# Moving the transposed activations to a pool behind the hidden tiles, at the weights' place modulo 4096 bytes

## The chip, the cores and the metric

The kernel runs on one core of one Trainium2 chip. The metric is the time of one execution on the device in microseconds. Three executions of the kernel before took 2161.57, 2165.28 and 2165.72 us; the median is 2165.28 us.

## The reference

Two layers of a hybrid block work on 256 tokens of width 2048, all in float32. Each layer does the following:

```python
h = rmsnorm(x, g_mix[l])
proj = h @ w_in[l]                       # 2048 -> 3904, split into seven parts
out_a = rglru_group(...)                 # gated linear recurrence, width 768
out_b = diff_attention_group(...)        # 4 heads, two softmaxes, width 512
out_c = mla_group(...)                   # 6 heads over a low-rank query and key/value, width 768
x = x + concatenate([out_a, out_b, out_c]) @ w_out[l]
h = rmsnorm(x, g_ffn[l])
x = x + (silu(h @ w_gate[l]) * (h @ w_up[l])) @ w_down[l]    # 2048 -> 5632 -> 2048
```

A last rmsnorm follows. Nearly all of the arithmetic is in the products with w_in, w_out, w_gate, w_up and w_down.

## The kernel before

**The split matmul.** Every float32 operand of a large product is held as two parts in the matmul format float32r: a high part, which is the rounded value, and a low part, which is the rest. A product is then three matmuls into one accumulator (`mm3`, lines 209 to 211): high by high, high by low, low by high. The first argument of `nc.tensor.matmul` after the accumulator is the stationary operand, loaded into the array, and the second one is the moving operand, which streams through it.

**The weights.** `load_split` (from line 187) brings a tile of up to 1024 columns of float32 per partition from HBM into one of three buffers of the pool wraw, on SyncE's queue. ScalarE rounds it into `whi` (line 203) and VectorE subtracts to get `wlo` (line 204); both are tiles of the pool whl, with three buffers each. A buffer is loaded again when both have read it.

**The activations.** `build_xT` transposes x on TensorE (line 283) in blocks of 128 by 128, scales it by the norm's gain and splits it into `xTh` and `xTl`, two tiles of 128 partitions by 16 k-slices by 256 tokens that live as long as the kernel. They lie in the pool `const`, between the small tile `half` and `junk`. The hidden activations, the mixed outputs and the normed low-rank inputs are split in the same way into `hTh` and `hTl`, tiles of 4 k-slices by 256 tokens (4096 bytes of a partition each), in the pool `ht` with six buffers of each.

**The order of the pools.** const comes first, then wraw, whl, ht and sm. Each pool follows the one before it in the partition's bytes. const holds ident, x, pv, half, xTh, xTl, junk, warm, pos_i, cst, rsb, the arena (17060 words) and some small tables.

**The products.** `gemm` uses the activations as the stationary side and streams the weights: for each weight tile, each half of 128 tokens, each segment of columns and each k-slice in the tile it issues `mm3`. Gate and up (`k2`) have two k-slices of 512 columns in a tile; w_out and w_down have one k-slice of 1024 columns as two segments of 512; the gemm at C_QA has one k-slice of 832 columns as 512 and 320; the one of w_q_b's rope columns has two k-slices of 384. Each of them gives twelve matmuls for a tile. `gemm_T` does the reverse: the weights are stationary in blocks of 128 columns, and the activations stream, 256 columns at a time. Its right side is xTh and xTl for the LRU's two inputs (768 columns each) and hTh and hTl for the attention's.

TensorE's program order is written out by hand: the generators in `side` and `lazy` (attention heads, transposes, recurrence) are given a turn after each weight tile by `tick`. The other engines' order comes from the scheduler, in which the weight casts and the evacuations have a high priority.

The products on xTh and xTl as the stationary side are the gemm at C_QA, the three at C_DQ, C_DQ + 512 and C_DV, and the eleven blocks of gate and up, in both layers. Those on hTh and hTl are w_out, w_down, the rope columns of w_q_b and the value columns of w_kv_b.

Of the kernel before, what the change touches and what calls it, by code (L numbers as in the profile page):

```python
# [11 lines left out]
F32 = mybir.dt.float32  # L12
F32R = mybir.dt.float32r
# [8 lines left out]
P = 128  # L22
D = 2048
T = 256
NT = 2
DEPTH = 2
KD = D // P
# [27 lines left out]
def body(ctx: ExitStack, tc: tile.TileContext, x_in, pos_in, pvec_in, lamv_in, cst_in, w_in, w_r, w_i, w_q_b,  # L55
         w_kv_b, w_out, w_gate, w_up, w_down, g_final, out):
    nc = tc.nc
    pool = lambda name, bufs=1, **k: ctx.enter_context(tc.tile_pool(name=name, bufs=bufs, **k))
    const = pool("const")
    wraw_p = pool("wraw", 3)  # L60
    whl_p = pool("whl", 3)
    ht_p = pool("ht", 6)
    sm_p = pool("sm", 4)
    acc_p = pool("acc", 5, space=PSUM)
    aux_p = pool("aux", 3, space=PSUM)
# [11 lines left out]
    load_x(0, 256)  # L77
    nc.sync.dma_start(pv, pvec_in)

    half = const.tile([P, 8], F32, name="half")  # L80
    xTh = const.tile([P, KD, T], F32R, name="xTh")
    xTl = const.tile([P, KD, T], F32R, name="xTl")
    junk = const.tile([P, 512], BF16, name="junk")
    warm = const.tile([P, 512], BF16, name="warm")
    nc.vector.memset(warm, 0.0)
    nc.gpsimd.memset(half, -0.5)
    nc.scalar.activation(junk[:, 0:8], half, AF.Exp)
    pos_i = const.tile([P, NT], I32, name="pos_i")
# [835 lines left out]
```

## Time and profile before

| | |
|---|---|
| median of three runs | 2165.28 us (2161.57 to 2165.72) |
| the profiled execution | 2164.01 us |
| its span, first to last instruction | 2162.2 us |
| mean granted TensorE clock | 0.997 of 2.4 GHz |
| TensorE matmul, busy | 2146.5 us (99%), 10302 instructions |
| TensorE weight load, busy | 1783.7 us (82%) |
| VectorE, busy | 1157.1 us (54%) |
| ScalarE, busy | 1003.4 us (46%) |
| moved by DMA | 391 MB, 181 GB/s on average |

The span is counted from the first to the last instruction; the execution's own time is 1.8 us longer. A matmul's duration in the trace runs from its start to the modelled end of its pipeline, so that matmuls overlap; the distance from one start to the next is the pace at which they are worked off. "PEclk" is the share of the full TensorE clock that was granted.

### The profile page before, as it was taken

How to read it: one execution, taken by the hardware profiler on the slowest of the kernel's cores; microseconds unless marked ns; L12 is line 12 of the kernel's file. 1: busy time of each engine (PE TensorE's matmuls, PEld its weight loads, DVE VectorE, ACT ScalarE, POOL GpSimd, SP SyncE). 2: the span in 40 equal slices, each digit the busy share in tenths (PEclk: the TensorE clock that was granted, in tenths of full speed). 3: DMA queues.
4: the chain of work that ended last, by engine and by line, in shares of the span. 5: the costliest groups of instructions: out<-in, count | busy, mean ns of one | idle time of the engine just before them, and what ended most of it. 6: DMA issues, size and time to landing. Idle time of an engine off the chain costs nothing.

```text
span 2162.2 us, 26714 instructions
## 1 busy us (share of the span) xinstructions
PE 2146.5 (99%) x10302; PEld 1783.7 (82%) x10302; DVE 1157.1 (54%) x1497; ACT 1003.4 (46%) x1345; POOL 12.9 (1%) x27
## 2 busy tenths in 40 slices
PE   9999999999999999999999999999999999999998
PEld 8888888888888888888898888888888888888886
DVE  5775755444444444444565757554444444445454
ACT  5764654444443344443447546454444433444443
POOL 0000000000000000000000000000000000000000
PEclk9999999999999999999999999999999999999999
DMA  7564456666665666666565645566666666666655
GB/s 216 172 166 131 151 176 185 185 185 184 185 189 192 193 186 186 185 186 191 181 189 158 180 126 184 178 179 190 182 185 187 191 193 189 186 187 181 189 184 171
DMA packets 183439, 391.14 MB, mean 181 GB/s; under 512 B 19088, under 2 KB 36624, under 8 KB 183184
## 3 DMA queue, kind: packets, MB, share of 16 engines
q1 hardware_dynamic: 183312, 389.45, 60.7%
q8 instruction: 80, 1.31, 0.3%
q14 instruction: 47, 0.39, 0.1%
HBM read 387.30 MB, written 2.10 MB: 180 GB/s over the span
## 4 chain that ended last, share of the span: by engine, by line
PE 98%; DMA 0%; issue 0%; ACT 0%; DVE 0%; SPq 0%; DVEq 0%; POOLq 0%; POOL 0%; ACTq 0%
PE acc L209 31%; PE acc L211 31%; PE acc L210 31%; PE aux L283 2%; PE aux L676 1%; PE aux L675 1%; PE aux L732 1%; DMA wraw<-in_w_in 0%; PE aux L690 0%; PE aux L534 0%; PE aux L533 0%; ACT whi L203 0%; PE aux L691 0%; SPq L75 0%; DVE wlo L204 0%
## 5 line engine op out<-in xcount | busy, mean ns | idle before, releaser
L204 DVE TENSOR_TENSOR wlo<-wraw,whi 128x1024 fp32r<-128x1024 f32 (+2 forms) x756 | 895.4, 1185 | 880.1 <-ACT whi L203 879.0
L203 ACT CAST whi<-wraw 128x1024 fp32r<-128x1024 f32 (+2 forms) x756 | 770.1, 1019 | 1053.4 <-PE acc L211 934.5
L209 PE MATMUL acc<-whi,xTh 128*128 128x512 f32 x1728 | 685.1, 396 | 1.8 <-ACT whi L203 1.0
L210 PE MATMUL acc<-wlo,xTh 128*128 128x512 f32 x1728 | 676.8, 392 | 0.6 <-DVE wlo L204 0.6
L211 PE MATMUL acc<-whi,xTl 128*128 128x512 f32 x1728 | 676.8, 392 | 0.0
L209 PE MATMUL acc<-whi,hTh 128*128 128x512 f32 (+1 forms) x992 | 388.6, 392 | 0.0
L209 PEld LDWEIGHTS acc<-whi,xTh 128*128 128x128 f32 x1728 | 326.1, 189 | 74.8 <-issue 1.3
L211 PEld LDWEIGHTS acc<-whi,xTl 128*128 128x128 f32 x1728 | 325.8, 189 | 73.4
L211 PE MATMUL acc<-whi,hTl 128*128 128x512 f32 (+1 forms) x992 | 385.5, 389 | 0.0
L210 PEld LDWEIGHTS acc<-wlo,xTh 128*128 128x128 f32 x1728 | 326.2, 189 | 71.4 <-DVE wlo L204 0.9
L210 PE MATMUL acc<-wlo,hTh 128*128 128x512 f32 (+1 forms) x992 | 384.8, 388 | 0.0
L209 PEld LDWEIGHTS acc<-whi,hTh 128*128 128x128 f32 x992 | 186.8, 188 | 38.1 <-issue 1.3
L211 PEld LDWEIGHTS acc<-whi,hTl 128*128 128x128 f32 x992 | 186.5, 188 | 38.0
L210 PEld LDWEIGHTS acc<-wlo,hTh 128*128 128x128 f32 x992 | 186.8, 188 | 36.9
L209 PE MATMUL acc<-xTh,whi 128*128 128x256 f32 x384 | 110.6, 288 | 0.2 <-ACT whi L203 0.2
L211 PE MATMUL acc<-xTh,wlo 128*128 128x256 f32 x384 | 108.4, 282 | 0.8 <-DVE wlo L204 0.8
L210 PE MATMUL acc<-xTl,whi 128*128 128x256 f32 x384 | 108.2, 282 | 0.6 <-DVE xTl L293 0.6
L209 PEld LDWEIGHTS acc<-xTh,whi 128*128 128x128 f32 x384 | 72.4, 188 | 2.7 <-issue 1.3
L210 PEld LDWEIGHTS acc<-xTl,whi 128*128 128x128 f32 x384 | 72.4, 189 | 1.1 <-DVE xTl L293 1.0
L211 PEld LDWEIGHTS acc<-xTh,wlo 128*128 128x128 f32 x384 | 72.3, 188 | 1.2 <-DVE wlo L204 1.2
L826 DVE SCALAR_TENSOR_TENSOR arena<-acc,rs,arena 128x512 f32<-128x512 f32 x44 | 32.9, 748 | 42.9 <-PE acc L211 42.9
L283 PE MATMUL aux<-ident,arena 128*128 128x128 f32 x324 | 48.6, 273 | 0.0
(174 smaller groups left out, 868.1 us busy)
## 6 DMA issues: line engine op xcount, KB each, us to landing
wraw<-in_w_gate SPq DMA_DIRECT2D x176, 512.0 KB, 3.7
wraw<-in_w_up SPq DMA_DIRECT2D x176, 512.0 KB, 3.7
wraw<-in_w_down SPq DMA_DIRECT2D x176, 512.0 KB, 4.5
wraw<-in_w_out SPq DMA_DIRECT2D x64, 512.0 KB, 3.8
wraw<-in_w_in SPq DMA_DIRECT2D x64, 384.0 KB, 3.2
wraw<-in_w_in SPq DMA_DIRECT2D x48, 512.0 KB, 3.8
wraw<-in_w_in SPq DMA_DIRECT2D x32, 416.0 KB, 3.4
wraw<-in_w_q_b SPq DMA_DIRECT2D x8, 384.0 KB, 4.0
```

The lines of the kernel that those rows point to most:

```text
L203: nc.scalar.copy(hi[:, :n], raw[:, :n])
L204: nc.vector.tensor_tensor(lo[:, :n], raw[:, :n], hi[:, :n].bitcast(F32), ALU.subtract)
L209: nc.tensor.matmul(ps, a[0], b[0], start=start, stop=False)
L210: nc.tensor.matmul(ps, a[0], b[1], start=False, stop=False)
L211: nc.tensor.matmul(ps, a[1], b[0], start=False, stop=stop)
L283: nc.tensor.transpose(ps[:, d:d + P], s, ident)
L675: nc.tensor.matmul(S[:, c0:c0 + n], qT[:, h, qs], kT[:, h, 0:n], start=True, stop=False)
L676: nc.tensor.matmul(S[:, c0:c0 + n], qrT[b0:b0 + 64, h // 2, qs], krT[b0:b0 + 64, 0:n], start=False, stop=True)
L732: nc.tensor.matmul(S[:, c0:c0 + n], qk[b0:b0 + 64, 0, q * P:(q + 1) * P], qk[b0:b0 + 64, 1, 0:n], start=True, stop=True)
L826: nc.vector.scalar_tensor_tensor(sil[t], ps, rs[0][:, t:t + 1], sil[t], ALU.mult, ALU.mult)
```

## The change

A new pool `xt`, with one buffer, is opened between ht and sm, and xTh and xTl are allocated from it instead of from const. The tile `half` is allocated a few lines later, after `warm`. No instruction is added or removed.

```diff
@@ -60,6 +60,7 @@
     wraw_p = pool("wraw", 3)
     whl_p = pool("whl", 3)
     ht_p = pool("ht", 6)
+    xt_p = pool("xt")
     sm_p = pool("sm", 4)
     acc_p = pool("acc", 5, space=PSUM)
     aux_p = pool("aux", 3, space=PSUM)
@@ -77,12 +78,12 @@
     load_x(0, 256)
     nc.sync.dma_start(pv, pvec_in)
 
-    half = const.tile([P, 8], F32, name="half")
-    xTh = const.tile([P, KD, T], F32R, name="xTh")
-    xTl = const.tile([P, KD, T], F32R, name="xTl")
+    xTh = xt_p.tile([P, KD, T], F32R, name="xTh")
+    xTl = xt_p.tile([P, KD, T], F32R, name="xTl")
     junk = const.tile([P, 512], BF16, name="junk")
     warm = const.tile([P, 512], BF16, name="warm")
     nc.vector.memset(warm, 0.0)
+    half = const.tile([P, 8], F32, name="half")
     nc.gpsimd.memset(half, -0.5)
     nc.scalar.activation(junk[:, 0:8], half, AF.Exp)
     pos_i = const.tile([P, NT], I32, name="pos_i")
```

## Rows read from the trace of the kernel before

**Rows 1.** The page, busy time by engine and the chain's shares by line.
```profile
PE 2146.5 (99%) x10302; PEld 1783.7 (82%) x10302; DVE 1157.1 (54%) x1497; ACT 1003.4 (46%) x1345; POOL 12.9 (1%) x27
...
PE acc L209 31%; PE acc L211 31%; PE acc L210 31%; PE aux L283 2%; PE aux L676 1%; PE aux L675 1%; PE aux L732 1%; DMA wraw<-in_w_in 0%; PE aux L690 0%; PE aux L534 0%; PE aux L533 0%; ACT whi L203 0%; PE aux L691 0%; SPq L75 0%; DVE wlo L204 0%
```
**Rows 2.** Groups by form, TensorE; names are out, moving, stationary; busy us, mean ns.
```profile
L209 PE MATMUL acc<-whi,xTh 128*128 128x512 f32 x1664 | 665.2, 400 | 1.8 <-ACT whi L203 1.0 <-DVE arena L487 0.8
L211 PE MATMUL acc<-whi,xTl 128*128 128x512 f32 x1664 | 657.0, 395 | 0.0
L210 PE MATMUL acc<-wlo,xTh 128*128 128x512 f32 x1664 | 656.8, 395 | 0.6 <-DVE wlo L204 0.6
L209 PE MATMUL acc<-whi,hTh 128*128 128x512 f32 x960 | 377.7, 393 | 0.0
L211 PE MATMUL acc<-whi,hTl 128*128 128x512 f32 x960 | 374.8, 390 | 0.0
L210 PE MATMUL acc<-wlo,hTh 128*128 128x512 f32 x960 | 374.1, 390 | 0.0
L209 PE MATMUL acc<-xTh,whi 128*128 128x256 f32 x384 | 110.6, 288 | 0.2 <-ACT whi L203 0.2
```
**Rows 3.** Timeline of gate and up, start and length in us; 156 matmuls, first and last.
```profile
355.90 0.40 PE L209 MATMUL acc<-whi,xTh 128*128 128x512 f32 x1
...
391.93 0.40 PE L211 MATMUL acc<-whi,xTl 128*128 128x512 f32 x1
```
**Rows 4.** Timeline of a down stretch; 486 matmuls, first and last.
```profile
630.07 0.39 PE L209 MATMUL acc<-whi,hTh 128*128 128x512 f32 x1
...
740.00 0.39 PE L211 MATMUL acc<-whi,hTl 128*128 128x512 f32 x1
```
**Rows 5.** Timeline of the gemm at C_QA; 36 matmuls before the last row.
```profile
55.28 0.39 PE L209 MATMUL acc<-whi,xTh 128*128 128x512 f32 x1
...
55.97 0.31 PE L209 MATMUL acc<-whi,xTh 128*128 128x320 f32 x1
...
56.41 0.39 PE L209 MATMUL acc<-whi,xTh 128*128 128x512 f32 x1
...
62.10 0.39 PE L209 MATMUL acc<-whi,xTh 128*128 128x512 f32 x1
```
**Rows 6.** Timeline of the gemm of w_q_b's rope columns; 24 matmuls, first and last.
```profile
117.32 0.34 PE L209 MATMUL acc<-whi,hTh 128*128 128x384 f32 x1
...
121.32 0.33 PE L211 MATMUL acc<-whi,hTl 128*128 128x384 f32 x1
```
**Rows 7.** Timeline, activations moving: 118 matmuls on xT, then 49 on hT.
```profile
1097.06 0.28 PE L209 MATMUL acc<-xTh,whi 128*128 128x256 f32 x1
...
1110.94 0.28 PE L209 MATMUL acc<-xTh,whi 128*128 128x256 f32 x1
...
1192.17 0.28 PE L210 MATMUL acc<-hTl,whi 128*128 128x256 f32 x1
...
1197.92 0.28 PE L210 MATMUL acc<-hTl,whi 128*128 128x256 f32 x1
```
**Rows 8.** The page's DMA issues: count, KB each, median us to landing.
```profile
wraw<-in_w_gate SPq DMA_DIRECT2D x176, 512.0 KB, 3.7
...
wraw<-in_w_down SPq DMA_DIRECT2D x176, 512.0 KB, 4.5
```
**Rows 9.** Stretches: us, busy of PE, PEld, DVE, ACT, POOL; PEclk, DMA share, GB/s.
```profile
630.00:740.00 110.00, 110.00 (x488) 91.06 (x486) 51.83 (x45) 42.46 (x41) 0.00 (x0) 1.00 0.61 192
445.00:484.00 39.00, 39.00 (x169) 31.61 (x168) 18.49 (x18) 15.96 (x16) 0.00 (x0) 1.00 0.62 180
```
**Rows 10.** Groups in gate and up, 445 to 484 us: the split of the weights.
```profile
L204 DVE TENSOR_TENSOR wlo<-wraw,whi 128x1024 fp32r<-128x1024 f32 x15 | 18.4, 1224 | 20.0 <-ACT whi L203 20.0
L203 ACT CAST whi<-wraw 128x1024 fp32r<-128x1024 f32 x14 | 14.7, 1049 | 22.0 <-PE acc L211 22.0
```
**Rows 11.** A stretch in the attention of the first layer, same columns as rows 9.
```profile
258.00:268.00 10.00, 9.21 (x34) 6.76 (x33) 7.42 (x26) 6.06 (x19) 0.00 (x0) 0.83 0.32 107
```

## The prediction

> **What bounds the kernel now.** I read the page from the top. TensorE is busy for 2146.5 of 2162.2 us, and the chain that ended last is almost only TensorE: three lines, the three products of the split matmul, hold 31% each [rows 1]. No wait stands on that path; the time is the number of matmuls times their pace, plus some 16 us of idle time. So the next view is the one that groups TensorE's work by form, and in it I look for equal shapes with unequal times. There is one pair. The 512-column matmuls whose stationary operand is a slice of xTh or xTl (3 x 1664 = 4992 of them) last 400, 395 and 395 ns; those of the same shape with hTh or hTl (3 x 960) last 393, 390 and 390 [rows 2]. These durations overlap, since matmuls are pipelined, so the pace has to be taken from the timeline, as start to start. In a gate and up stretch with nothing between, the first starts at 355.90 us and the 156th at 391.93: 36.03 us over 155 steps, 232.4 ns each [rows 3]. In a down stretch, 630.07 to 740.00 us are 485 steps: 226.7 ns each [rows 4]. The granted clock is 1.00, the 2.4 GHz level, in stretches of both kinds [rows 9]. So equal work costs 5.7 ns (2.5%) more when xT is the stationary side.
>
> **Is it the stage or the operand?** The two stretches differ in more than the operand: gate and up take two k-blocks of 512 columns per weight tile and give six matmuls in a row to one accumulator, down takes one k-block of 1024 columns and changes the accumulator after three. Two other stages cross this. The first gemm after the LRU input (C_QA, 832 columns as 512 and 320) has down's order with xT: from 55.28 to 62.10 us go six rounds of three 512-column and three 320-column matmuls, 6.82 us or 1.137 us a round. Three of the narrow ones take 56.41 - 55.97 = 0.44 us, which leaves 0.697 us for three wide ones: 232.2 ns each, slow [rows 5]. The gemm of w_q_b has gate's order, two k-blocks a tile, with hT and 384 columns: 4.00 us over 23 steps, 173.9 ns [rows 6]. From 384 to 512 columns at one column per 1/2.4 ns are 53.3 ns more, 227.2 ns: the fast pace. So the order of the stage does not make the pace; the operand goes with it, and what tells xT from hT to TensorE is where it lies.
>
> **Where it lies.** By my count of the allocations (bytes of a partition): ident 512, x 16384, pv 696 and half 32 lie ahead of xTh, so it starts some 1.2 KB past a multiple of 4096. The constants end near 122.7 thousand, some 3.9 KB past one, and there begin wraw (3 x 4096), whl (6 x 4096) and ht (12 x 4096), all whole multiples. So hTh and hTl have the remainder of whi and wlo, and xTh and xTl one about 2.7 KB off. The change takes 32768 bytes, 8 x 4096, out of the constants, so that wraw, whl, ht and the arena keep their remainders, and xT follows ht on the weights' remainder, in bytes (176 to 209 thousand) where hT slots lie now. A slice of 1024 bytes per k, 512 per half of the tokens, gives xT the eight places within 4096 that hT's four k-slices have; the moving sides start at 0 or 2048 in both. Down pairs all eight with both at one pace.
>
> **The sum.**
> - 512-column matmuls on xT: 4992 x (232.4 - 226.7) = 28.5 us less [rows 2 to 4]. The grouped durations give 1664 x (7 + 5 + 5) ns = 28.3 us, a second count from other numbers [rows 2]. Lower end: gate and up alone gain (2 layers x 11 blocks x 16 x 2 x 2 x 3 = 4224), and 5 ns each: 21 us. Upper end: 6.2 ns each, 31 us, half a nanosecond beyond hT's pace; no row shows a lower one.
> - 320 columns, 192 of them: now 146.7 ns [rows 5], and the fast 173.9 ns less 64 columns at 1/2.4 ns is 147.2 [rows 6]. They are on the fast pace already: 0, either end 0.1 us.
> - xT as the moving side, 3 x 384 matmuls of 256 columns [rows 2]: 13.88 us over 117 steps, 118.6 ns, against 119.8 with hT (5.75 us over 48 steps) [rows 7]. Here xT's present place is the better one. If it becomes like hT, 1152 x 1.2 = 1.4 us are lost; the other end is 1.4 us gained, the same difference the other way. I take the loss.
> - The transposes and attention matmuls read x, ident and arena. Their remainders stay (junk and warm alone move by 32 bytes against them), so 0. Were their distance in whole 4096s to count like xT's place, 2.5% of the 2% of the chain in L283 [rows 1] is 1.1 us either way.
> - The builders of xT write the same bytes to another address, and `half` is allocated after warm but filled at the same point: 0, with the first stage's weight wait as cover.
> - What is late next. All of the gain is taken off TensorE, so the weights must come 2.5% faster in gate and up. A 512 KB tile feeds 12 matmuls: 2.79 us now, 2.72 us then. A raw buffer must be filled, cast and subtracted within three tiles, 8.16 us: 3.7 us to landing [rows 8], 1.05 us and 1.22 us [rows 10] leave 2.2 us. The cast's only idle time there, 22.0 us, is ended by TensorE [rows 10], that is, the weights wait for it. Down lives at 2.72 us a tile with 4.5 us to landing [rows 8] and 192 GB/s, where gate and up use 180 [rows 9]. So 0, and what it costs if that fails stands under the rivals. In the attention stages the side work has 0.07 us less per tile; I give it up to 1 us of new idle time, from the 16 us there are.
>
> 28.5 - 1.4 - 0.3 (a part of that last 1 us) = 26.8, say 27 us. The profiled execution took 2164.0 us, 1.8 more than its span; 2164.0 - 27 = 2137 us. It lies 1.3 us under the median of the runs, 2165.28, within their spread of 4 us.
>
> The trace also speaks against a rule here: same shape, same clock, 5.7 ns apart by operand. The Trainium skill, "SBUF — State Buffer", section "SBUF: two separate sides", says of the engines' ports that contention is confined to the pair which VectorE and GpSimd share, and "PE, ACT, and DVE's dedicated pair never wait on anyone." By that rule an address could not cost TensorE anything and the time would stay at 2164; by the rows it does cost.
>
> **The rivals.**
> - *The place does nothing* (2164, chance 0.07). Every slow wide matmul belongs to an xT stage, so something else of those stages could slow the stream: the shorter rows of the weights' transfers, or the activations on ScalarE. For it: no single row shows an address. Against it: the slow pace in the first gemm, which has neither up-projection nor Silu [rows 5]. The port rule of the Trainium skill named above would be this case.
> - *The distance counts too* (2150, chance 0.06). After the move xT lies 13 to 25 times 4096 past the slots of the weights' parts (it lies behind ht's twelve), and hT lay 1 to 17 times past them. If only about half of these distances is fast, half of 28.5 us stays: 2164 - 14 = 2150. Against it: down uses six slots of each part, spread over that whole stretch, at one pace [rows 4].
> - *The weights come late* (slower, 2174, chance 0.04). Place: gate and up, where a row of a transfer is half as long as in down. If a tile's landing takes over 2.2 us longer than now, TensorE idles at the block's start, and an idle stretch can be followed by the 1.2 GHz level: at 258 to 268 us the engine idles for 0.8 us and the granted clock is 0.83 over 10 us [rows 11], 1.7 us lost. One such fall in each of the 22 gate and up blocks costs 37 us: 2164 - 27 + 37 = 2174. It decides against the change from 16 falls on. Against it: the 2.2 us, and a share of the transfer engines of 0.62 here and 0.61 in down [rows 9].
> - *The pool does not land where the words say* (chance 0.03). If a pool started on some other remainder, xT would have a new place with a pace of its own: 2164 if it is as bad as now, more if worse.
>
> **How the numbers follow.** Forecast 0.80; its own range is 2133 to 2141 (31 us less; 22 us less and a clock fall more). The others 0.07, 0.06, 0.04 and 0.03. To leave out no more than 2 in 10 the range goes from 2133 to 2147, which takes in partial gains of 17 us. A measurement here tells about 0.2%, 4.3 us, from no change. Faster: 0.80 + 0.06 = 0.86; within: 0.07 + 0.02 = 0.09; slower: 0.04 + 0.01 = 0.05.
>
> **What would show it.** Right: in the group view, the xT wide matmuls at 393, 390 and 390 ns like hT's; start to start 226.7 ns in gate and up, with no interval of 0.24 us left; the first gemm's round at 1.120 us instead of 1.137; hT stages unchanged; gate and up at some 185 GB/s or more, with the cast still waiting for TensorE. The 256-column stream at 119.8 ns shows the loss of 1.4 us, at 118.6 it did not come. Wrong: the wide xT matmuls still at 232 ns (the place is not the cause), a mixture of both paces by slice (distance), or the casts waiting for DMA and new stretches at the lower clock (late weights).

## The result and the profile after

The changed kernel takes 2139.59 us (median of four runs, 2138.23 to 2141.62) against 2164.28 us before on the same chip. The ratio is 0.989, with a 95% interval of 0.9878 to 0.9903: 24.7 us or 1.1% faster. The forecast was 2137 us, with a range of 2133 to 2147. The profiled execution took 2138.23 us with a span of 2136.4, that is 25.8 us less than 2164.01 and 2162.2 before.

The page after, busy time and the chain by line, to be read against [rows 1]. Lines of the code are one higher than before, so L210 to L212 are the three products of the split matmul.

```profile
PE 2121.6 (99%) x10302; PEld 1780.3 (83%) x10302; DVE 1157.0 (54%) x1497; ACT 1004.1 (47%) x1345; POOL 12.9 (1%) x27
...
PE acc L210 31%; PE acc L212 31%; PE acc L211 31%; PE aux L284 2%; DMA wraw<-in_w_in 1%; PE aux L677 1%; PE aux L676 1%; PE aux L733 1%; PE aux L691 0%; PE aux L534 0%; PE aux L535 0%; ACT whi L204 0%; DMA x<-in_x 0%; ACT junk L311 0%; DVE wlo L205 0%
```

TensorE lost 24.9 us of busy time with the same 10302 instructions. The idle part of the span went from 15.7 to 14.8 us. VectorE and ScalarE are as they were. The same chain, then, and each link of it shorter.

The groups by form after, in the columns of [rows 2]:

```profile
L210 PE MATMUL acc<-whi,xTh 128*128 128x512 f32 x1664 | 657.0, 395 | 1.1 <-DVE arena L488 0.8 <-ACT whi L204 0.4
L212 PE MATMUL acc<-whi,xTl 128*128 128x512 f32 x1664 | 649.0, 390 | 0.0
L211 PE MATMUL acc<-wlo,xTh 128*128 128x512 f32 x1664 | 648.0, 389 | 0.6 <-DVE wlo L205 0.6
L210 PE MATMUL acc<-whi,hTh 128*128 128x512 f32 x960 | 377.6, 393 | 0.0
L212 PE MATMUL acc<-whi,hTl 128*128 128x512 f32 x960 | 374.7, 390 | 0.0
L211 PE MATMUL acc<-wlo,hTh 128*128 128x512 f32 x960 | 374.3, 390 | 0.0
L210 PE MATMUL acc<-xTh,whi 128*128 128x256 f32 x384 | 111.0, 289 | 0.2 <-ACT whi L204 0.2
```

The three xT lines fell from 400, 395 and 395 ns to 395, 390 and 389. The three hT lines did not move. The sum of the xT lines' busy time fell from 1979.0 to 1954.0 us. The stream of 256 columns, where xT moves, went the other way, 110.6 to 111.0 us in this line, and its three lines together from 327.2 to 328.7 us.

The timeline after, the first and the last of 216 matmuls of a gate and up stretch, answers to [rows 3]:

```profile
738.67 0.39 PE L210 MATMUL acc<-whi,xTh 128*128 128x512 f32 x1
...
787.40 0.39 PE L212 MATMUL acc<-whi,xTl 128*128 128x512 f32 x1
```

48.73 us over 215 steps are 226.7 ns a step, down's pace to the tenth [rows 4].

The gemm at C_QA after; the last row begins the seventh round, as in [rows 5]:

```profile
53.15 0.39 PE L210 MATMUL acc<-whi,xTh 128*128 128x512 f32 x1
...
53.85 0.30 PE L210 MATMUL acc<-whi,xTh 128*128 128x320 f32 x1
...
54.27 0.39 PE L210 MATMUL acc<-whi,xTh 128*128 128x512 f32 x1
...
59.91 0.39 PE L210 MATMUL acc<-whi,xTh 128*128 128x512 f32 x1
```

Six rounds take 6.76 us, 1.127 us each instead of 1.137. That is a gain, but 10 ns where three wide matmuls should have given 17. Nor is it the wide ones' gain: three of them take 0.70 us up to the first narrow one, against 0.69 us in [rows 5], and by the start times of all six rounds their mean step is 232.4 ns before and after. The narrow ones went from 146.9 to 143.1 ns.

Gate and up has such slow steps too, behind the transposes that its blocks let in. Here are the second and the eleventh wide matmul behind four transposes:

```profile
390.78 0.39 PE L211 MATMUL acc<-wlo,xTh 128*128 128x512 f32 x1
...
392.86 0.39 PE L211 MATMUL acc<-wlo,xTh 128*128 128x512 f32 x1
```

These nine steps take 2.08 us, 231.1 ns each. By the start times of this trace, the first ten steps behind each of the 22 groups of transposes in a layer's gate and up are off the pace (the first takes 315 ns, the other nine 231.2 ns on average), and every later one takes 226 or 227 ns until the next group. At C_QA the width changes after every three matmuls, so the pace may never settle there; no run tests that.

A stretch of gate and up after, in the columns of [rows 9]:

```profile
740.00:787.00 47.00, 47.00 (x209) 38.91 (x208) 23.20 (x21) 19.19 (x19) 0.00 (x0) 1.00 0.67 191
```

And the cast of the weights in that stretch, as in [rows 10]:

```profile
L204 ACT CAST whi<-wraw 128x1024 fp32r<-128x1024 f32 x17 | 17.9, 1054 | 26.1 <-PE acc L212 24.4 <-DVE wlo L205 1.7
```

Gate and up now draw 191 GB/s. The cast still waits for TensorE (24.4 of 26.1 us) and never for a transfer.

Ten microseconds each around the end of the LRU's first gemm and in the first layer's attention, after; the second answers to [rows 11], and the column to read is PEclk:

```profile
45.00:55.00 10.00, 8.30 (x49) 6.84 (x48) 7.23 (x17) 3.55 (x4) 0.00 (x0) 1.00 0.62 190
255.00:265.00 10.00, 9.21 (x34) 6.74 (x33) 6.88 (x26) 5.54 (x18) 0.00 (x0) 0.83 0.36 107
```

The kernel before had two such falls, the other one at 47 to 57 us:

```profile
47.00:57.00 10.00, 7.66 (x32) 6.06 (x31) 8.00 (x20) 3.94 (x5) 0.00 (x0) 0.83 0.53 162
```

TensorE idles at that place in both profiles (7.66 and 8.30 us busy of 10), and only one of them shows the fall. In another profile of the changed kernel (run e11_after_again) it comes at 47 to 57 us, 0.83, and not at 258 to 268 us, 1.00. A clock of 0.83 over 10 us costs 1.7 us at most. So up to 1.7 of the profiled 25.8 us are not the change's; the rest agrees with the 24.7 us of the medians.

### The profile page after: what moved, and what is told of

The parts are those of the page before. It is cut to its first block, busy times and chain, and to the rows that moved or that the text cites. A ratio compares the mean times of both kernels' runs of the same rounds, so it can differ in the third digit from the quotient of the medians.

```text
span 2136.4 us, 26714 instructions
## 1 busy us (share of the span) xinstructions
PE 2121.6 (99%) x10302; PEld 1780.3 (83%) x10302; DVE 1157.0 (54%) x1497; ACT 1004.1 (47%) x1345; POOL 12.9 (1%) x27
## 4 chain that ended last, share of the span: by engine, by line
PE 98%; DMA 1%; issue 0%; ACT 0%; DVE 0%; SPq 0%; DVEq 0%; POOLq 0%; POOL 0%; ACTq 0%
PE acc L210 31%; PE acc L212 31%; PE acc L211 31%; PE aux L284 2%; DMA wraw<-in_w_in 1%; PE aux L677 1%; PE aux L676 1%; PE aux L733 1%; PE aux L691 0%; PE aux L534 0%; PE aux L535 0%; ACT whi L204 0%; DMA x<-in_x 0%; ACT junk L311 0%; DVE wlo L205 0%
## 5 line engine op out<-in xcount | busy, mean ns | idle before, releaser
L210 PE MATMUL acc<-whi,xTh 128*128 128x512 f32 x1728 | 676.6, 392 | 1.1 <-DVE arena L488 0.8
L212 PE MATMUL acc<-whi,xTl 128*128 128x512 f32 x1728 | 668.5, 387 | 0.0
L211 PE MATMUL acc<-wlo,xTh 128*128 128x512 f32 x1728 | 667.7, 386 | 0.6 <-DVE wlo L205 0.6
L210 PE MATMUL acc<-whi,hTh 128*128 128x512 f32 (+1 forms) x992 | 388.5, 392 | 0.0
L212 PE MATMUL acc<-whi,hTl 128*128 128x512 f32 (+1 forms) x992 | 385.5, 389 | 0.0
L210 PEld LDWEIGHTS acc<-whi,xTh 128*128 128x128 f32 x1728 | 324.5, 188 | 66.7 <-issue 1.3
L212 PEld LDWEIGHTS acc<-whi,xTl 128*128 128x128 f32 x1728 | 324.4, 188 | 66.4
L212 PEld LDWEIGHTS acc<-whi,hTl 128*128 128x128 f32 x992 | 186.6, 188 | 38.4
L210 PEld LDWEIGHTS acc<-whi,hTh 128*128 128x128 f32 x992 | 186.8, 188 | 37.8 <-issue 1.3
L210 PE MATMUL acc<-xTh,whi 128*128 128x256 f32 x384 | 111.0, 289 | 0.2 <-ACT whi L204 0.2
L212 PE MATMUL acc<-xTh,wlo 128*128 128x256 f32 x384 | 108.9, 284 | 0.7 <-DVE wlo L205 0.7
L210 PEld LDWEIGHTS acc<-xTh,whi 128*128 128x128 f32 x384 | 73.5, 191 | 2.5 <-issue 1.3
L212 PEld LDWEIGHTS acc<-xTh,wlo 128*128 128x128 f32 x384 | 73.4, 191 | 1.1 <-DVE wlo L205 1.1
```

The lines of the kernel that those rows point to most:

```text
L210: nc.tensor.matmul(ps, a[0], b[0], start=start, stop=False)
L211: nc.tensor.matmul(ps, a[0], b[1], start=False, stop=False)
L212: nc.tensor.matmul(ps, a[1], b[0], start=False, stop=stop)
```

## The experiments

All are built on the changed kernel or on the one before by moving tiles; none leaves out work. Theory A says that the pace depends on the distance between the slice that is stationary and the weights that stream, modulo something that divides 4096; B takes that modulus as 4096; C says that the region of the memory counts; D says that xT's own place counts. Distances below are from the programs' allocations, in bytes of a partition.

**The weights moved to xT.** In the kernel before, xT left where it is:

```diff
     lamt = const.tile([P, DEPTH], F32, name="lamt")
+    const.tile([P, 96], F32, name="gapc")
```

> The kernel before, with 384 unused bytes at the end of the constants, so that wraw, whl and ht move and xT stays among the constants. xT then lies 1024 bytes past the weights' parts modulo 4096, that is 0 modulo 512; its own place is unchanged. Theory A (what counts is the distance of the stationary slice from the streamed weights modulo 512 or a part of it): xT's wide matmuls at 226.7 ns instead of 232.4, about 2138 us. Theory B (it is the distance modulo 4096): slow, 2164. Theory C (it is the region: among the constants slow, behind ht fast): 2164. Theory D (it is xT's own remainder, whatever the weights'): 2164.

Measured: 2139.55 us, ratio 0.9888 (0.9873 to 0.9902). Two groups by form of this run, one of xT and one of hT:

```profile
L210 PE MATMUL acc<-wlo,xTh 128*128 128x512 f32 x1664 | 648.3, 390 | 0.6 <-DVE wlo L204 0.6
...
L210 PE MATMUL acc<-wlo,hTh 128*128 128x512 f32 x960 | 374.1, 390 | 0.0
```

The whole gain came with xT at its old address, among the constants, 1024 bytes off the weights modulo 4096. B, C and D fall; 384 unused bytes do what the new pool does.

**xT behind ht, but off the weights' place.** In the changed kernel:

```diff
+    xt_p.tile([P, 96], F32, name="gapx")
     xTh = xt_p.tile([P, KD, T], F32R, name="xTh")
```

> The changed kernel, with 384 unused bytes ahead of xTh in the new pool: xT lies behind ht, but 384 bytes past the weights' place modulo 512, as before the change. Theory A and theory B: xT's wide matmuls back at 232.4 ns, about 2164 to 2166 us. Theory C (region): 2139. Theory D: slow as well, since xT's own remainder modulo 512 (352) is that of before; only the first run tells A from D.

Measured: 2163.28 us, ratio 1.0 (0.9991 to 1.0009). The same two groups:

```profile
L212 PE MATMUL acc<-wlo,xTh 128*128 128x512 f32 x1664 | 656.8, 395 | 0.6 <-DVE wlo L206 0.6
...
L212 PE MATMUL acc<-wlo,hTh 128*128 128x512 f32 x960 | 374.2, 390 | 0.0
```

The pool alone brings nothing; xT's line is back at 395 ns. The two runs together show the place relative to the weights as the cause, in both directions.

**Everything moved by 32 bytes.** In the changed kernel:

```diff
     lamt = const.tile([P, DEPTH], F32, name="lamt")
+    const.tile([P, 8], F32, name="gapc")
```

> The changed kernel, with 32 unused bytes at the end of the constants: wraw, whl, ht and xT all start at 0 modulo 4096 instead of 4064, their distances unchanged. Theories A to C: 2139 us, hT and xT both at 226.7 ns. Theory D: another pace for xT and hT alike, either way.

Measured: 2139.17 us, ratio 0.9885 (0.9869 to 0.9902). The absolute place, 4064 or 0 modulo 4096, does not count.

**hT moved off, xT left on.** In the changed kernel:

```diff
+    ht_p.tile([P, 96], F32, name="gaph", bufs=1)
+    xt_p.tile([P, 32], F32, name="gapx")
     xTh = xt_p.tile([P, KD, T], F32R, name="xTh")
```

> The changed kernel with 384 unused bytes ahead of hTh and 128 more ahead of xTh: now the hidden tiles lie 384 bytes off the weights' place modulo 512, and xT lies on it (512 off). Theory A: hT's 2880 wide matmuls slow down by 5 to 5.7 ns, 14 to 16 us, xT's stay at 227: 2154 to 2156 us. Rival (something else of hT's stages makes them fast): 2139.5.

Measured: 2155.3 us (2153.8 to 2156.2), ratio 0.9961 (0.9947 to 0.9975) to the kernel before. The groups by form, xT's low part and then hT:

```profile
L214 PE MATMUL acc<-whi,xTl 128*128 128x512 f32 x1664 | 649.5, 390 | 0.0
...
L212 PE MATMUL acc<-whi,hTh 128*128 128x512 f32 x960 | 382.4, 398 | 0.0
L214 PE MATMUL acc<-whi,hTl 128*128 128x512 f32 x960 | 379.6, 395 | 0.0
L213 PE MATMUL acc<-wlo,hTh 128*128 128x512 f32 x960 | 379.3, 395 | 0.0
```

Now hT has the 398, 395 and 395 ns of a misplaced operand, in stages that were never slow before, and xT keeps 390. 2880 x 5 ns = 14 us by these means; 2155.3 - 2139.6 = 15.7. This is the crossing that the prediction tried to read from two odd gemms.

**A sweep in steps of 64 bytes.** In the changed kernel xT is cut into eight tiles, each of two k-slices and 64 spare bytes:

```diff
-    xTh = xt_p.tile([P, KD, T], F32R, name="xTh")
+    xTh = [xt_p.tile([P, 2 * T + 16], F32R, name="xTh" + c) for c in "ABCDEFGH"]
...
-        return xTh[:, k, :], xTl[:, k, :]
+        s = slice(k % 2 * T, (k % 2 + 1) * T)
+        return xTh[k // 2][:, s], xTl[k // 2][:, s]
```

> The changed kernel, with xTh and xTl cut into eight tiles A to H of two k-slices, each 64 bytes further from the weights' place modulo 512 than the one before (A at 0, B at 64, ... H at 448). By the kernel before, 384 (G) gives about 395 ns as the mean duration of a wide matmul in the low-part lines; by the changed one, 0 (A) gives 390. Theory A: the tiles differ by name in one run, A at 390 and G at 395, and the others say whether the step is 128, 256 or 512 bytes. Theory C: all at 390. If A holds and half of the tiles are slow: about 2139 + 13 = 2152 us.

Measured: 2154.9 us (one run). The second product's groups by form for the eight tiles; A lies on the weights' place, B 64 bytes past it, and so on:

```profile
L211 PE MATMUL acc<-wlo,xThF 128*128 128x512 f32 x208 | 82.2, 395 | 0.0
...
L211 PE MATMUL acc<-wlo,xThB 128*128 128x512 f32 x208 | 82.1, 395 | 0.0
...
L211 PE MATMUL acc<-wlo,xThC 128*128 128x512 f32 x208 | 82.1, 395 | 0.0
...
L211 PE MATMUL acc<-wlo,xThG 128*128 128x512 f32 x208 | 82.1, 395 | 0.0
...
L211 PE MATMUL acc<-wlo,xThA 128*128 128x512 f32 x208 | 81.6, 392 | 0.6 <-DVE wlo L205 0.6
...
L211 PE MATMUL acc<-wlo,xThD 128*128 128x512 f32 x208 | 81.2, 390 | 0.0
...
L211 PE MATMUL acc<-wlo,xThE 128*128 128x512 f32 x208 | 81.1, 390 | 0.0
...
L211 PE MATMUL acc<-wlo,xThH 128*128 128x512 f32 x208 | 81.0, 389 | 0.0
```

E, 256 bytes off, is as fast as hT, which has 389 ns in this line of this run. B, C, F and G lie 64 or 128 bytes past a multiple of 256 and are slow. D and H, 192 bytes past one, are as fast as E in this line but not in the other two: 396 and 397 ns against 393 in the first product, 393 against 390 in the third. From start to start among matmuls of the same shape, E goes at 227.4 ns, D and H at 229.8 and 229.6, and B, C, F and G at 232.2 to 233.3. Tiles 256 bytes apart agree, so the distance counts modulo 256; of the four places 0 is the fastest, and 192 costs at most half of what 64 and 128 cost. A carries the blocks' first matmuls with their waits, and B, which holds the second pair of slices, the matmuls beside transposes (413 ns in the first product), so that the means of these two are not their place's alone.

**The sweep in steps of 32 bytes.** As before with `2 * T + 8`.

> The sweep again with steps of 32 bytes: A at 0, B at 32, ... H at 224 past the weights' place modulo 256 (the eight steps of 64 bytes repeated after four). A as 0 (390 ns in the low-part lines), C as 64, E as 128 (395), G as 192. New are B, D, F and H. Theory A with a unit of 64 bytes: each like its lower neighbour, or between its neighbours, about 2153 us. If one is under 226.7 ns from start to start, the best place is not the weights' own.

Measured: 2161.97 us (one run). Groups by form of the second product: hT on the weights' place, then tiles at 0, 32, 96 and 224 bytes:

```profile
L211 PE MATMUL acc<-wlo,hTh 128*128 128x512 f32 x960 | 373.6, 389 | 0.0
...
L211 PE MATMUL acc<-wlo,xThA 128*128 128x512 f32 x208 | 81.8, 393 | 0.6 <-DVE wlo L205 0.6
L211 PE MATMUL acc<-wlo,xThB 128*128 128x512 f32 x208 | 82.1, 395 | 0.0
...
L211 PE MATMUL acc<-wlo,xThD 128*128 128x512 f32 x208 | 82.4, 396 | 0.0
...
L211 PE MATMUL acc<-wlo,xThH 128*128 128x512 f32 x208 | 82.1, 395 | 0.0
```

The new places, with 395 and 396 ns against hT's 389, are no better than 128 bytes, and the kernel is 9 us slower than expected. From start to start the four new places (32, 96, 160 and 224 bytes) go at 232.9 to 233.8 ns, and G, at 192, at 229.4. (A, at 0, again carries the blocks' first matmuls; from start to start it has 228.2 ns.) So H, at 224 bytes (233.1 ns), is slower than both of its neighbours, and a unit of 64 bytes, the expectation's premise, does not hold. A misplacement of 32 bytes costs like one of 128; no multiple of 32 is better than 0.

**xTl alone off.** In the changed kernel:

```diff
     xTh = xt_p.tile([P, KD, T], F32R, name="xTh")
+    xt_p.tile([P, 96], F32, name="gapx")
     xTl = xt_p.tile([P, KD, T], F32R, name="xTl")
```

> The changed kernel with 384 unused bytes between xTh and xTl, so that the low part alone lies off the weights' place. Its slices are loaded while wlo streams past xTh, and stream whi themselves. Theory A1 (the load of the next slice against the stream under way): the steps that begin with the line of wlo and xTh take some 232 ns, the others 227. Theory A2 (a slice against its own stream): the line of xTl takes 232. Both: a third of 26 us comes back, about 2148 us.

Measured: 2156.32 us (one run). The groups by form, in the order of their busy time:

```profile
L213 PE MATMUL acc<-whi,xTl 128*128 128x512 f32 x1664 | 660.2, 397 | 0.0
L212 PE MATMUL acc<-wlo,xTh 128*128 128x512 f32 x1664 | 658.7, 396 | 0.6 <-DVE wlo L206 0.6
L211 PE MATMUL acc<-whi,xTh 128*128 128x512 f32 x1664 | 656.8, 395 | 1.6 <-ACT whi L205 0.9 <-DVE arena L489 0.8
```

The line during which xTl is loaded (396 against 389) and the line that streams past it (397 against 390) are both slow; the third is fast (395, as after). So one misplaced slice hits two steps, and 17 us come back instead of the 8 to 9 of either theory alone.

**wlo alone off.** In the changed kernel the low part's tile begins 128 bytes into a wider buffer:

```diff
-        lo = whl_p.tile([P, CHUNK], F32R, name="wlo")
+        lo = whl_p.tile([P, CHUNK + 64], F32R, name="wlo")[:, 32:]
```

> The changed kernel with the low part of the weights 128 bytes off the place of everything else modulo 256, in all stages (xT and hT stay on whi's place). Only the stream of wlo is misplaced, against both the slice it streams past and the one loaded meanwhile. With xTl off, two of the three steps were slow, 5.3 and 6.8 ns. If the two conflicts of one stream do not add: the line of wlo at 232 ns for xT and hT alike, the others at 227: (1664 + 960) x 5.5 ns = 14 us, 2154 us. If they add: 12 ns, 31 us, 2171 us. If it takes the high part: no change, 2139.5.

Measured: 2176.91 us (one run), slower than the kernel before. The groups by form of xT, and the first one of hT:

```profile
L210 PE MATMUL acc<-whi,xTh 128*128 128x512 f32 x1664 | 666.2, 400 | 2.2 <-ACT whi L204 1.8 <-DVE arena L488 0.5
L212 PE MATMUL acc<-whi,xTl 128*128 128x512 f32 x1664 | 655.3, 394 | 0.0
L211 PE MATMUL acc<-wlo,xTh 128*128 128x512 f32 x1664 | 655.1, 394 | 0.6 <-DVE wlo L205 0.6
L210 PE MATMUL acc<-whi,hTh 128*128 128x512 f32 x960 | 382.7, 399 | 0.0
```

All three expectations missed: the time is past the "they add" case, and not one line but all three are slow (400, 394, 394 against 395, 390, 389). One misplaced part of the weights spoils the whole triple, in xT's and hT's stages alike (hT's three lines have 399, 394 and 393 ns against 393, 390 and 390). Which step pays for which conflict is therefore not settled.

**The narrow stream put at a distance of its own.** The sweep had a second result. In the stages where xT moves and the weights are stationary, 256 columns wide, its distances gave these groups by form (A, whose means hold waits, and C, with 283 ns, left out):

```profile
L211 PE MATMUL acc<-xTlG,whi 128*128 128x256 f32 x48 | 13.6, 284 | 0.0
...
L211 PE MATMUL acc<-xTlE,whi 128*128 128x256 f32 x48 | 13.5, 282 | 0.0
L211 PE MATMUL acc<-xTlD,whi 128*128 128x256 f32 x48 | 13.5, 280 | 0.6 <-DVE xTlD L295 0.6
L211 PE MATMUL acc<-xTlH,whi 128*128 128x256 f32 x48 | 13.4, 280 | 0.0
...
L211 PE MATMUL acc<-xTlF,whi 128*128 128x256 f32 x48 | 13.4, 279 | 0.0
...
L211 PE MATMUL acc<-xTlB,whi 128*128 128x256 f32 x48 | 13.3, 278 | 0.0
```

E, at a multiple of 256, is not the best here; the odd multiples of 64, B, D, F and H, are better by 2 to 6 ns. From start to start D and H go at 115.0 and 117.0 ns, B and F at 116.2 and 117.9, and C, E and G at 118.6 to 119.5. I took the place of D and H, by writing the weights 64 bytes further into their buffers for these stages alone:

```diff
-    def load_split(src_ap, kk, shape):
+    def load_split(src_ap, kk, shape, o=0):
...
+            hi, lo = hi[:, o:o + n], lo[:, o:o + n]
...
-            hi, lo = load_split(w[k * P:(k + 1) * P], 1, w.shape[1:])
+            hi, lo = load_split(w[k * P:(k + 1) * P], 1, w.shape[1:], 16)
```

> The changed kernel; where the weights are the stationary side (gemm_T), their parts are written 64 bytes further into their buffers, so that the streamed activations lie 64 bytes before them modulo 256. In the sweep the tiles D and H, which have this distance, streamed at 115 to 117 ns a matmul of 256 columns, A and E at 119 to 120. Theory A (place of the loaded slice against the streamed one): 1152 + 216 matmuls x 3 to 5 ns, 4 to 7 us less than the changed kernel: 2133 to 2136. Rival: these stages are paced by the weights' transfers or by the weight loads, which need their 188 ns each: no change, 2139.5.

Measured: 2135.67 us (2134.32 to 2138.84), ratio 0.9873 (0.9858 to 0.9888). Since its interval overlaps the changed kernel's, both were measured again, on one chip:

> The changed kernel again, beside the next one on the same chip: 2139.5 us.

> The kernel with gemm_T's weights 64 bytes further in, again: by theory A 4 to 6 us (0.2 to 0.3%) under the changed kernel of the same call, about 2135 us; if the first result was spread between runs, 2139.5.

Measured: 2140.66 us (2139.34 to 2142.01), ratio 0.9894 (0.9878 to 0.9911), for the changed kernel; 2134.14 us (2132.64 to 2135.51), ratio 0.9863 (0.9848 to 0.9877), for this one. The four runs of each do not overlap; the difference is 6.5 us, 0.3%. The timeline of the LRU's first gemm of the second layer, the first and last of 126 matmuls, first in the changed kernel:

```profile
1082.17 0.36 PE L210 MATMUL acc<-xTh,whi 128*128 128x256 f32 x1
...
1097.25 0.28 PE L212 MATMUL acc<-xTh,wlo 128*128 128x256 f32 x1
```

and in this one:

```profile
1080.08 0.37 PE L211 MATMUL acc<-xTh,whi 128*128 128x256 f32 x1
...
1094.37 0.28 PE L213 MATMUL acc<-xTh,wlo 128*128 128x256 f32 x1
```

15.08 us against 14.29 us over 125 steps: 120.6 and 114.3 ns. It is the fastest version here.

## Why the prediction was right

- *The wide matmuls on xT, 28.5 us.* The mechanism held: 232.4 became 226.7 ns. The size was 25.0 us by the busy time of the three lines (1979.0 to 1954.0), which includes what the missing fall of the clock gave the gemm at C_QA, 1.7 us at most. The clean stretches' difference of 5.7 ns was applied to all 4992. By the start times it is 5.2 ns over gate and up's 4224 (22.1 us), where the steps behind transposes gained less; 3.9 ns over the 576 at C_DQ, C_DQ + 512 and C_DV (2.2 us); and 0.7 ns over the 96 at C_QA in the second layer, where neither profile shows a fall of the clock. The 3.5 us between 28.5 and 25.0 are the largest error of the sum; the forecast lies 2.6 us under the median of the runs. The lower end, 21 us, was the more useful bound.
- *The second count from durations, 28.3 us,* took differences of rounded means. From the busy columns of [rows 2], 1979.0 less 1664/960 of hT's 1126.6 us, it is 26.2 us, and 25.0 came.
- *The stage or the operand.* The conclusion was right for gate and up and the attention's gemms, but one of its two proofs was not. At C_QA the wide matmuls go at 232.4 ns on the old place and on the new one, so their slow pace there was no sign of the place. The run with hT moved off is the proof that was wanted.
- *Where it lies.* The distances came out as counted: xT was 2688 bytes off the weights modulo 4096, now 0. The count leaves out 16512 bytes that lie ahead of ident, so each place is 128 bytes further past a multiple of 4096 than it says, which no distance feels. But 4096 was more than is needed. The moduli 4096 and 256 were open, since hT's slices and the moving sides only show multiples of 512; the first run decided against 4096, and the sweep for 256.
- *The 320-column matmuls at 0.* They were not on their fast pace yet: from 146.9 to 143.1 ns at C_QA is 0.7 us for all 192, a small gain that the sum did not have.
- *The loss of 1.4 us on the 256-column ones.* It came, 1.5 us by the busy time of the three lines, and the pace after is 120.6 ns in a stretch that begins with a longer step. That this stream wants another distance was in the rows, and the prediction took it as a cost to be borne; the last version takes it as 6 us to be had.
- *The signs.* Two of those named did not come, both for the same reason: steps of 0.24 us are left, behind transposes and at C_QA, and the round at C_QA takes 1.127 us and not 1.120.
- *What is late next.* Nothing: 191 GB/s in gate and up, the cast still released by TensorE. The rival of late weights did not show, nor that of a pool landing elsewhere. "The distance counts too" is refuted by gate and up, whose tiles use all the buffers: past the tenth step behind transposes every one takes 226 or 227 ns.
- *The place does nothing* is refuted by the first two runs. The Trainium skill, "SBUF — State Buffer", section "SBUF: two separate sides", has it that TensorE's port never waits on anyone; 384 bytes of padding that change 2139.6 us into 2163.3 us say that TensorE's pace depends on where its own two operands lie. The other users of the memory do not explain it: in the trace of the kernel before, 29 wide xT steps fall in times without work on ScalarE, VectorE and GpSimd, and 257 in times without a DMA packet under way, each counted from 250 ns before its start, and they take 233.4 and 232.4 ns. What contends inside the memory, and why the best distance differs with the width, no run here shows.

## What to carry to other kernels

Where TensorE is the bound, compare equal matmul shapes across stages by their start to start distance; a few nanoseconds between them are worth a percent, and the operands' addresses are a cause that no wait in the profile shows. Place the stationary and the streaming operand of wide float32r matmuls at the same remainder modulo 256 bytes, which a few unused bytes behind the constants can do, and all parts of a split matmul alike, since one misplaced part slowed two or all three of its steps. Try the distance anew for each width: 0 was best at 512 columns, and 64 bytes was better than 0 at 256. Expect the gain in long runs of one width only: it was absent from the wide matmuls where 512 and 320 columns alternate.

## What the runs showed of the hardware

- The pace of 512-column float32r matmuls at 2.4 GHz depends on the distance of the stationary from the streaming operand modulo 256 bytes: 226.7 ns at 0, 232.4 ns at 128, about 229.6 ns at 192, and 32 bytes are already enough to lose it (395 against hT's 389 ns in mean duration). The absolute place (4064, 0 or 352 modulo 4096), the region and higher bits of the distance did not count.
- The fast pace comes only after some steps: behind transposes the first ten wide steps are off it, the last nine of them at 231.2 ns on average, at a granted clock of 1.00. Why, no run shows.
- At 256 columns a distance of 64 bytes (weights past activations) gave 114.3 ns against 120.6 ns at 0; 192 bytes was nearly as good in the sweep and was not tried alone.
- A misplaced low part of the weights alone made the kernel slower (2176.9 us) than xT wholly misplaced (2163.3 us), as it spoils hT's stages too. A misplaced xTl slowed the step that loads it and the step that uses it. Why the cost of these parts does not follow step by step stays open.
